# A mixture-of-experts kernel: one gather buffer, a scatter in native float32, 21 weight buffers for 19

## The chip, the core and the metric

One core of a Trainium2 chip. The metric is device time in microseconds (us), the median of several executions of the whole kernel. The engines named below are TensorE (PE in the rows; its weight loads are PEld), VectorE (DVE), ScalarE (ACT), GpSimd (POOL) and SyncE (SP), which issues nearly all of the weight transfers.

## What is computed

256 tokens of width 1024 go through two blocks. The first is attention (two kinds, merged through gates) and then a mixture of 32 experts. The second is three kinds of attention and a dense MLP. The change touches the mixture and the two rows that scale the first block's branches:

```python
mod_x = (jax.nn.silu(c) @ w_ada[l] + b_ada[l])[:, None, :]
sh_a, sc_a, g_a, sh_m, sc_m, g_m = jnp.split(mod_x, N_MOD, axis=-1)
x = x + g_a * _merge(ya, yb, ga, gb, w_oa[l], w_ob[l], w_out[l])
hx = _modulate(_rmsnorm(x, norm_mlp[l]), sh_m, sc_m)
x = x + g_m * moe(hx)
# moe: each token goes to 4 of the 32 experts, weighted by a softmax of its 4 largest logits
gate = jnp.minimum(xe @ w_gate[e] + b_gate[e], SWIGLU_LIMIT)
up = jnp.clip(xe @ w_up[e] + b_up[e], -SWIGLU_LIMIT, SWIGLU_LIMIT)
act = (up + 1) * (gate * jax.nn.sigmoid(SWIGLU_ALPHA * gate))
yb = act @ w_down[e] + b_down[e]
y = segment_sum(yb * weight, token)
```

Every expert has three matrices of 1024 x 1024 float32. All 96 of them are read, 4 MB each.

## The kernel before

The first block's attention fills the span up to about 300 us, the experts follow to about 1226 us, and the second block takes the rest. The function `moe()` holds the experts, two at a time: 16 pairs. Each expert has 64 slots for tokens, so the 128 rows of a PSUM bank hold two experts, the first in the array's columns 0 to 63, the second in 64 to 127 (`ab` = 0 and 1). What does not fit in 64 slots is done by `overflow()`, a branch behind pair 6 (`OVER_AT`) that these inputs do not enter, but whose count SyncE and the others have to read.

A weight tile is 1 MB, and a pair needs 24: eight each for gate, up and down. The tiles live in a ring of `SLOTS` = 12 buffers and in `EXTRA` = 7 more that exist only while the experts run. `fill()` issues a transfer (L206) as soon as a buffer is given back; which buffer that is, and which transfer, is fixed when the program is built.

For each pair `p` the loop at the end of `moe()` writes: `gate(p)`; the scatter of pair p-2; `prep1` and `prep2` of pair p+1; `up(p)`; `prep3` of pair p+1; `down(p-1)`; `trans(p)`. `prep1` builds a 0/1 matrix (scaled) on VectorE, and `prep2` gathers with it: 16 native float32 matmuls of 128 columns (L1291) put the pair's tokens into PSUM, and 4 ScalarE and 4 VectorE instructions (L1299, L1296) apply the norm and write the tile `xg`, which has two buffers. `prep3` transposes the 0/1 matrix (L1308) into the scatter's matrix `sc`, and finds the slots' weights `ws` (L1313). `expert_mm` (L1381) runs gate, up and down: for one pair of weight tiles it issues eight matmuls of 64 x 512, alternately in the one half of the array and in the other. Such a group of eight is called a block here; a pair has 12. Gate's and up's bias is a small matmul ahead (L1372).

`gate` clips (VectorE L1398), takes the sigmoid (ScalarE L1399) into a scratch tile of the name `e2` and multiplies (L1400). `up` clips into a scratch tile (L1409), and then adds one and multiplies (L1410). Down's result is split by ScalarE and VectorE (`split_out`, L513 and L514) into a rounded high part and the rest, and `scatter` (L1464, L1465) adds both with two matmuls in the reduced type float32r to the sum of the tokens, `acc`, for two halves of the tokens and two of the width: 8 matmuls of 128 x 512 for a pair. `acc` holds four of the eight PSUM banks from start to end; the other four rotate.

`tc.issue_after` and a scheduler settle the order on each engine: gathers and scatters are put between the matmuls of a block where their inputs are expected to be ready, so the order of the source is not that of the engine.

The row `gm_b` (g_m, copied to all partitions) is made during attention by `ada_one` and `bcast_rows` (L683 to L685), beside `ga_b`, and is used once, behind the experts (L1609).

## Time and profile before

| what | us |
|---|---|
| median of 3 runs (1702.76 to 1704.06) | 1703.26 |
| the profiled execution | 1698.37 |
| its span in the trace | 1696.6 |
| TensorE busy in it | 1621.6 (96%) |
| VectorE busy | 695.2 (41%) |
| ScalarE busy | 466.0 (27%) |
| experts, first gate bias to the last of them (in the trace) | 301.73 to about 1226 |

The profiled execution is 4.9 us below the median, and its span is 1.77 us shorter than its own time. The times in the rows below are of that span. "Busy" of TensorE contains time in which only one half of the array works, so 96% does not say that it could not go faster. A bracket in a row by time is idle time of the engine just before, and what ended it.

### The profile page before, as it was taken

How to read it: one execution, taken by the hardware profiler on the slowest of the kernel's cores; microseconds unless marked ns; L12 is line 12 of the kernel's file. 1: busy time of each engine (PE TensorE's matmuls, PEld its weight loads, DVE VectorE, ACT ScalarE, POOL GpSimd, SP SyncE). 2: the span in 40 equal slices, each digit the busy share in tenths (PEclk: the TensorE clock that was granted, in tenths of full speed). 3: DMA queues.
4: the chain of work that ended last, by engine and by line, in shares of the span. 5: the costliest groups of instructions: out<-in, count | busy, mean ns of one | idle time of the engine just before them, and what ended most of it. 6: DMA issues, size and time to landing. Idle time of an engine off the chain costs nothing. (4 is left out here: it accounts for less than half of the span.)

```text
span 1696.6 us, 22129 instructions
## 1 busy us (share of the span) xinstructions
PE 1621.6 (96%) x9024; PEld 1012.3 (60%) x9024; DVE 695.2 (41%) x1348; ACT 466.0 (27%) x768; POOL 81.8 (5%) x112
## 2 busy tenths in 40 slices
PE   5999899999999999899999999999999999999997
PEld 3777797544434443354344334433388899989996
DVE  4898986311121111221211111111267556665555
ACT  3435564101000100110000001000256445454443
POOL 2102100000000000000000000000004101100001
PEclk9999999999999999999999999999999999999999
DMA  9643588999999999999999999999973433565540
GB/s 344 260 154 141 202 282 335 382 425 425 426 426 425 425 425 426 382 425 425 425 426 425 425 426 426 426 422 424 405 277 102 146 121 131 178 218 184 176 153 25
DMA packets 117035, 537.42 MB, mean 317 GB/s; under 512 B 11666, under 2 KB 13438, under 8 KB 66754
## 3 DMA queue, kind: packets, MB, share of 16 engines
q1 hardware_dynamic: 112144, 532.19, 78.4%
q10 hardware_dynamic: 4610, 3.52, 0.7%
q8 instruction: 72, 1.18, 0.3%
q0 software_dynamic: 176, 0.26, 0.1%
q14 instruction: 33, 0.27, 0.0%
HBM read 534.88 MB, written 1.05 MB: 316 GB/s over the span
## 5 line engine op out<-in xcount | busy, mean ns | idle before, releaser
L1381 PE MATMUL bank_a<-w,xg 128*64 128x512 f32 x2048 | 522.5, 599 | 2.2 <-DMA w<-in_w_up_dram 2.2
L1381 PEld LDWEIGHTS bank_a<-w,xg 128*64 128x64 f32 x2048 | 182.7, 137 | 280.9 <-issue 258.5
L319 DVE TENSOR_TENSOR wl<-w,wh 128x1024 fp32r<-128x1024 f32 (+1 forms) x193 | 236.2, 1228 | 153.0 <-ACT wh L316 145.1
L316 ACT ACTIVATE wh<-w 128x1024 fp32r<-128x1024 f32 (+1 forms) x193 | 202.1, 1049 | 220.1 <-PE bank_a L389 98.7
L1381 PE MATMUL bank_a<-w,at 128*64 128x512 f32 x960 | 228.4, 595 | 6.5 <-DVE e L1409 5.0
L390 PE MATMUL bank_a<-hi,wl 128*128 128x256 f32 x640 | 180.3, 283 | 1.0 <-DVE wl L319 1.0
L388 PE MATMUL bank_a<-hi,wh 128*128 128x256 f32 x616 | 176.3, 287 | 1.1 <-ACT hi L474 0.6
L389 PE MATMUL bank_a<-lo,wh 128*128 128x256 f32 x616 | 174.3, 283 | 0.2 <-DVE lo L475 0.2
L1381 PEld LDWEIGHTS bank_a<-w,at 128*64 128x64 f32 x960 | 83.5, 137 | 146.6 <-issue 102.9
L513 ACT ACTIVATE y<-bank_a,ws 128x512 fp32r<-128x512 f32 x32 | 22.0, 687 | 443.1 <-PE bank_a L1381 429.9
L390 PEld LDWEIGHTS bank_a<-hi,wl 128*128 128x128 f32 x640 | 122.3, 192 | 1.4 <-DVE wl L319 1.4
L388 PEld LDWEIGHTS bank_a<-hi,wh 128*128 128x128 f32 x616 | 117.8, 192 | 3.2 <-issue 0.9
L389 PEld LDWEIGHTS bank_a<-lo,wh 128*128 128x128 f32 x616 | 118.1, 192 | 0.9 <-DVE lo L475 0.6
L514 DVE SCALAR_TENSOR_TENSOR y<-bank_a,ws,y 128x512 fp32r<-128x512 f32 x32 | 24.0, 751 | 217.9 <-ACT y L513 216.2
L1409 DVE TENSOR_SCALAR e<-bank_a 128x512 f32<-128x512 f32 x32 | 22.1, 691 | 187.1 <-PE bank_a L1381 185.9
L1399 ACT ACTIVATE e<-gs 128x512 f32<-128x512 f32 x32 | 20.2, 630 | 236.7 <-DVE gs L1398 225.2
L1291 PEld LDWEIGHTS bank_a<-gr,x_sb 128*128 128x128 f32 x512 | 64.2, 196 | 23.0 <-issue 19.5
L1398 DVE TENSOR_SCALAR gs<-bank_a 128x512 f32<-128x512 f32 x32 | 22.0, 691 | 131.2 <-PE bank_a L1381 115.8
L1291 PE MATMUL bank_a<-gr,x_sb 128*128 128x128 f32 x512 | 69.3, 286 | 0.7 <-DVE gr L1274 0.7
L1296 DVE TENSOR_SCALAR xg<-bank_a,abp 128x128 f32<-128x128 f32 x64 | 21.9, 404 | 107.7 <-PE bank_a L1291 107.5
L1299 ACT ACTIVATE xg<-bank_a,abp 128x128 f32<-128x128 f32 x64 | 24.2, 455 | 121.8 <-PE bank_a L1291 121.7
L354 PE MATMUL bank_b<-wh,hh 128*128 128x512 f32 x128 | 49.9, 390 | 0.0
(453 smaller groups left out, 2198.4 us busy)
## 6 DMA issues: line engine op xcount, KB each, us to landing
w<-in_w_up_dram SPq DMA_DIRECT2D x144, 1024.0 KB
w<-in_w_down_dram SPq DMA_DIRECT2D x136, 1024.0 KB
w<-in_w_gate_dram SPq DMA_DIRECT2D x128, 1024.0 KB
w<-in_w_in_dram SPq DMA_DIRECT2D x45, 1024.0 KB
w<-in_w_ada_dram SPq DMA_DIRECT2D x16, 1024.0 KB
w<-in_w_ada_dram SPq DMA_DIRECT2D x16, 512.0 KB
w<-in_w_out_dram SPq DMA_DIRECT2D x8, 1024.0 KB
w<-in_w_down_dram SPq DMA_DIRECT2D x16, 512.0 KB
```

The costliest lines, as they stand in the source:

```text
L316: split_last[0] = S.activation(r32(wh[:, :n]), t[:, o:o + n], AF.Copy)
L319: V.tensor_tensor(r32(wl[:, :n]), t[:, o:o + n], wh[:, :n], op=OP.subtract)
L354: PE.matmul(o, r32(sh), r32(mh), start=first, stop=False)
L388: PE.matmul(o, r32(wh[:, k, c]), r32(hi[:, j]), start=j == 0 and m % 2 == 0, stop=False)
L389: PE.matmul(o, r32(wh[:, k, c]), r32(lo[:, j]), start=False, stop=False)
L390: PE.matmul(o, r32(wl[:, k, c]), r32(hi[:, j]), start=False, stop=j == 7 and m % 2 == 1)
L513: S.activation(r32(hi), src, AF.Copy, scale=scale)
L514: V.scalar_tensor_tensor(out=r32(lo), in0=src, scalar=scale, in1=hi, op0=OP.mult, op1=OP.subtract)
L1291: PE.matmul(ps[:, k], x_sb[:, tt, o:o + 255:2], d["gr"][:, tt].rearrange("p e s -> p (e s)"), start=tt == 0, stop=tt == 1)
L1299: S.activation(xg[:, j], ps[:, k], AF.Identity, bias=abp_[:, 1, j:j + 1], scale=abp_[:, 0, j:j + 1])
L1381: state["mm"] = PE.matmul(ps[h][64 * ab:64 * ab + 64], lhs(j, ab), w[ab][:, e, 512 * h:512 * h + 512], start=bias is None and j == 0, stop ...
L1409: V.tensor_scalar(out=u_, in0=ps[h], scalar1=7.0, scalar2=-7.0, op0=OP.min, op1=OP.max)
```

## The change

- `EXTRA` goes from 7 to 9: 21 weight buffers while the experts run.
- The room comes from smaller scratch. `xg` has one buffer. The `e2` tiles are gone: gate's sigmoid is written back into its PSUM bank, and so is up's clip. `gm_b` is no longer kept from attention to the end.
- With one `xg`, the next pair's gather may not be written before `up(p)` has read the present one, so `prep1`, `prep2` and `prep3` of pair p+1 are written behind `up(p)` (behind `overflow()` for pair 6).
- `down_out` writes one float32 tile for a pair, half of it by ScalarE and half by VectorE, and `scatter` is one native float32 matmul where it was two of float32r: 4 for a pair.
- `gate_rows`, behind the experts, makes g_m's row anew: 8 native float32 matmuls of 128 x 128, 8 VectorE instructions ahead of them and 2 ScalarE copies behind. During attention, four matmuls and two copies for it are left out.
- Scratch pools of `overflow()` are rearranged.

```diff
-EXTRA = 7
+EXTRA = 9
...
-            xg = m2.tile([128, 8, 2 * CAP], F32, name="xg", tag="xg")
+            xg = m1.tile([128, 8, 2 * CAP], F32, name="xg", tag="xg")
...
-                s_ = m1.tile([128, 512], F32, name="e2", tag="e2")
                 V.tensor_scalar(out=g_, in0=ps[h], scalar1=7.0, scalar2=None, op0=OP.min)
-                S.activation(s_, g_, AF.Sigmoid, scale=1.702)
-                V.tensor_tensor(g_, g_, s_, op=OP.mult)
+                S.activation(ps[h], g_, AF.Sigmoid, scale=1.702)
+                V.tensor_tensor(g_, g_, ps[h], op=OP.mult)
...
-                V.tensor_scalar(out=u_, in0=ps[h], scalar1=7.0, scalar2=-7.0, op0=OP.min, op1=OP.max)
-                V.scalar_tensor_tensor(out=g_, in0=u_, scalar=1.0, in1=g_, op0=OP.add, op1=OP.mult)
+                V.tensor_scalar(out=ps[h], in0=ps[h], scalar1=7.0, scalar2=-7.0, op0=OP.min, op1=OP.max)
+                V.scalar_tensor_tensor(out=g_, in0=ps[h], scalar=1.0, in1=g_, op0=OP.add, op1=OP.mult)
...
         def down_out(p, h, ps):
-            y = scr([128, 1024], "y", "wl")
-            yh, yl = y[:, 0:512], y[:, 512:1024]
-            split_out(yh, yl, ps, pairs[p]["ws"])
-            state["y", p, h] = (yh, yl)
+            if ("ybuf", p) not in state:
+                state["ybuf", p] = scr([128, 1024], "y", "wl")
+            y = state["y", p, h] = state["ybuf", p][:, 512 * h:512 * h + 512]
+            ws = pairs[p]["ws"]
+            if h:
+                V.tensor_scalar(out=y, in0=ps, scalar1=ws, scalar2=None, op0=OP.mult)
+            else:
+                S.activation(y, ps, AF.Copy, scale=ws)
...
-                yh, yl = state.pop(("y", p, h))
+                y = state.pop(("y", p, h))
                 for tt in range(2):
-                    st_ = r32(sc[:, 128 * tt:128 * tt + 128])
-                    PE.matmul(acc[tt][h], st_, r32(yh), start=False, stop=False)
-                    PE.matmul(acc[tt][h], st_, r32(yl), start=False, stop=p == NPAIR - 1)
+                    PE.matmul(acc[tt][h], sc[:, 128 * tt:128 * tt + 128], y, start=False, stop=p == NPAIR - 1)
...
-            if p + 1 < NPAIR:
-                prep1(p + 1)
-                prep2(p + 1)
             if p == 0:
                 prep3(0)
             up(p)
-            if p + 1 < NPAIR:
+            if p + 1 < NPAIR and p != OVER_AT:
+                prep1(p + 1)
+                prep2(p + 1)
                 prep3(p + 1)
...
+                prep1(p + 1)
+                prep2(p + 1)
+                prep3(p + 1)
...
+        def gate_rows(h):
+            ps = bank("a", shape=(128, 4, 128))
+            for i in range(4):
+                dg = rest[:, h, 128 * i:128 * i + 128]
+                V.tensor_scalar(out=dg, in0=ident, scalar1=mod[:, 2, i, 2 + h, 0:1], scalar2=None, op0=OP.mult)
+                PE.matmul(ps[:, i], ones, dg, start=i == 0, stop=i == 3)
+            S.copy(gm_b[:, 512 * h:512 * h + 512], ps.rearrange("p i n -> p (i n)"))
```

TensorE, a pair in the middle of the experts (pair 3 to 5, 9 or later), from the end of the gate's bias. `w,xg` are gate's and up's matmuls, `y,sc` scatters, `gr,x_sb` gathers. Before:

```order
L1381 MATMUL bank_a<-w,xg 64x512 x2
L1464 MATMUL bank_b<-y,sc 128x512
L1381 MATMUL bank_a<-w,xg 64x512 x6
L1465 MATMUL bank_b<-y,sc 128x512
L1464 MATMUL bank_b<-y,sc 128x512
L1465 MATMUL bank_b<-y,sc 128x512
L1291 MATMUL bank_a<-gr,x_sb 128x128 x3
L1381 MATMUL bank_a<-w,xg 64x512 x2
L1291 MATMUL bank_a<-gr,x_sb 128x128 x7
L1381 MATMUL bank_a<-w,xg 64x512 x6
L1291 MATMUL bank_a<-gr,x_sb 128x128 x6
L1381 MATMUL bank_a<-w,xg 64x512 x2
```

In the changed kernel, the same stretch, the gate's first two blocks:

```order
L1377 MATMUL bank_a<-w,xg 64x512 x2
L1461 MATMUL bank_b<-y,sc 128x512
L1377 MATMUL bank_a<-w,xg 64x512 x6
L1461 MATMUL bank_b<-y,sc 128x512 x2
L1377 MATMUL bank_a<-w,xg 64x512 x2
```

and the rest of gate and up, from behind up's bias matmuls to prep3's first transpose (`kh,gb`):

```order
L1377 MATMUL bank_a<-w,xg 64x512 x24
L1287 MATMUL bank_a<-gr,x_sb 128x128 x7
L1377 MATMUL bank_a<-w,xg 64x512 x6
L1287 MATMUL bank_a<-gr,x_sb 128x128 x6
L1377 MATMUL bank_a<-w,xg 64x512 x2
L1287 MATMUL bank_a<-gr,x_sb 128x128 x3
L1377 MATMUL bank_a<-w,xg 64x512 x22
L1304 LDWEIGHTS gb
L1304 MATMUL bank_a<-kh,gb 128x128
```

The scatter still stands inside gate's first block, one matmul where there were two. Of the 16 gathers, seven stood inside one block (gate's second) and nine between blocks; now seven stand inside up's first block, three inside its second and six between them. Each time they stand between two matmuls of one half of the array and two of the other. Prep3 has moved from between gate and up to between up and down.

VectorE, the end of up and the begin of down in such a pair: L1409 and L1410 are up's clip and product, L514 is down's result. Before:

```order
L1409 TENSOR_SCALAR e_4079<-bank_a 128x512
L1410 SCALAR_TENSOR_TENSOR gs<-e_4079,gs 128x512
L1409 TENSOR_SCALAR e_4082<-bank_a 128x512
L1410 SCALAR_TENSOR_TENSOR gs<-e_4082,gs 128x512
L514 SCALAR_TENSOR_TENSOR y<-bank_a,ws,y 128x512 x2
L1317 TENSOR_REDUCE ws<-bank_a 64x1 x2
L1310 CAST sc<-bank_a 128x256
```

In the changed kernel (L1403 and L1404 are up's clip and product, L1292 the gather's write of `xg`, L1424 half of down's result):

```order
L1403 TENSOR_SCALAR bank_a<-bank_a 128x512
L1404 SCALAR_TENSOR_TENSOR gs<-bank_a,gs 128x512
L1403 TENSOR_SCALAR bank_a<-bank_a 128x512
L1292 TENSOR_SCALAR xg<-bank_a,abp 128x128
L1404 SCALAR_TENSOR_TENSOR gs<-bank_a,gs 128x512
L1292 TENSOR_SCALAR xg<-bank_a,abp 128x128 x3
L1273 TENSOR_TENSOR gb<-kc,pos 128x256
L1424 TENSOR_SCALAR y<-bank_a,ws 128x512
L1313 TENSOR_REDUCE ws<-bank_a 64x1 x2
L1306 CAST sc<-bank_a 128x256
```

The four writes of `xg` now stand among up's clip and product, ahead of everything that prep3 and down give VectorE.

## Rows read from the trace of the kernel before

**Rows 1.** Page, part 2: GB/s moved, 40 equal slices of the span.
```profile
GB/s 344 260 154 141 202 282 335 382 425 425 426 426 425 425 425 426 382 425 425 425 426 425 425 426 426 426 422 424 405 277 102 146 121 131 178 218 184 176 153 25
```

**Rows 2.** By windows: length; busy and counts of PE, PEld, DVE, ACT, POOL; clock; DMA; GB/s.
```profile
301.73:389.69 87.96, 86.50 (x434) 42.39 (x434) 21.17 (x54) 9.82 (x18) 0.00 (x0) 0.98 0.97 405
389.69:448.69 59.00, 57.94 (x255) 23.77 (x254) 10.28 (x22) 5.31 (x10) 0.00 (x0) 1.00 1.01 425
448.69:506.93 58.24, 57.18 (x255) 23.25 (x254) 10.28 (x22) 5.31 (x10) 0.00 (x0) 1.00 1.01 425
623.44:688.63 65.19, 58.18 (x258) 23.89 (x257) 10.14 (x21) 5.89 (x11) 0.00 (x0) 0.99 1.01 425
688.63:849.68 161.05, 159.91 (x753) 71.65 (x753) 31.22 (x70) 15.23 (x29) 0.00 (x0) 0.98 0.99 414
849.68:1143.17 293.49, 287.85 (x1261) 117.77 (x1261) 49.83 (x104) 26.54 (x50) 0.00 (x0) 1.00 1.01 425
```

**Rows 3.** By windows: two stretches of 10 us with little transfer.
```profile
300.00:310.00 10.00, 10.00 (x58) 4.50 (x58) 3.58 (x14) 2.14 (x4) 0.00 (x0) 1.00 0.66 247
700.00:710.00 10.00, 10.00 (x64) 5.96 (x62) 3.25 (x6) 2.65 (x6) 0.00 (x0) 1.00 0.63 243
```

**Rows 4.** Waits of SyncE's DMA queue, 310 to 680 us: total us, times, longest.
```profile
SPq L206 <- PE bank_a L1381: 231.4, 98, 8.4
```

**Rows 5.** TensorE by time, one pair: start, us, line, tile, count, [idle before].
```profile
456.54 1.93 PE L1381 MATMUL bank_a<-w,xg 128*64 128x512 f32 x4
458.40 1.92 PE L1291 MATMUL bank_a<-gr,x_sb 128*128 128x128 f32 x14
460.25 3.65 PE L1381 MATMUL bank_a<-w,xg 128*64 128x512 f32 x12
...
474.17 0.28 PE L1308 MATMUL bank_a<-kh,gb 128*128 128x128 bf16 x2
475.02 0.25 PE L1313 MATMUL bank_a<-w,gb 128*128 128x96 bf16 x2 [0.56 <-DVE gs L1398]
475.19 14.01 PE L1381 MATMUL bank_a<-w,xg 128*64 128x512 f32 x64
489.13 1.07 PE L1381 MATMUL bank_a<-w,at 128*64 128x512 f32 x2
490.65 13.95 PE L1381 MATMUL bank_a<-w,at 128*64 128x512 f32 x62 [0.45 <-DVE e L1409]
504.53 0.73 PE L1464 MATMUL bank_b<-y,sc 128*128 128x512 f32 x2
```

**Rows 6.** TensorE by time near the end of the experts.
```profile
1201.02 3.69 PE L1359 MATMUL bank_b<-bd,wtt 32*128 32x512 f32 x8
1204.64 0.50 PE L1464 MATMUL bank_b<-y,sc 128*128 128x512 f32 x1
1204.97 0.39 PE L1465 MATMUL bank_b<-y,sc 128*128 128x512 f32 x1
1205.20 0.39 PE L1464 MATMUL bank_b<-y,sc 128*128 128x512 f32 x1
1205.43 0.40 PE L1465 MATMUL bank_b<-y,sc 128*128 128x512 f32 x1
```

**Rows 7.** VectorE by time where up ends and down begins.
```profile
488.38 0.69 DVE L1409 TENSOR_SCALAR e<-bank_a 128x512 f32<-128x512 f32 x1 [11.43 <-PE bank_a L1381]
...
490.63 0.69 DVE L1410 SCALAR_TENSOR_TENSOR gs<-e,gs 128x512 f32<-128x512 f32 x1
```

**Rows 8.** Instructions by line and form, 400 to 640 us: busy, mean ns.
```profile
L514 DVE SCALAR_TENSOR_TENSOR y<-bank_a,ws,y 128x512 fp32r<-128x512 f32 x8 | 6.0, 751 | 53.2 <-ACT y L513 52.7
...
L1296 DVE TENSOR_SCALAR xg<-bank_a,abp 128x128 f32<-128x128 f32 x16 | 5.5, 404 | 38.7 <-PE bank_a L1291 38.7
```

**Rows 9.** TensorE by time, first matmul after the overflow's branch.
```profile
688.63 1.06 PE L1372 MATMUL bank_a<-b_gate,sel 96*64 96x512 bf16 x4 [5.95 <-PEq L1473]
```

**Rows 10.** TensorE by time, the last pair's waits for weights (two of four).
```profile
1177.75 2.79 PE L1381 MATMUL bank_a<-w,xg 128*64 128x512 f32 x10 [1.65 <-DMA w<-in_w_up_dram]
...
1197.44 2.79 PE L1381 MATMUL bank_a<-w,at 128*64 128x512 f32 x10 [0.61 <-DMA w<-in_w_down_dram]
```

More of the change, by code (lines that the diff above doesn't have):

```diff
@@ L430, in build @@
     mod = keep.tile([128, 3, 4, 4, 2], F32, name="mod")
-    gm_b = keep.tile([128, D], F32, name="gm_b")
     kc = keep.tile([128, 256], F32, name="kc")
@@ L527, in body @@
         ga_b = p1.tile([128, D], F32, name="ga_b")
+        gm_s = p1.tile([128, D], F32, name="gm_s")
         rwa = p1.tile([128, 8, 32], F32, name="rwa")
@@ L620, in ada_one @@
             w = live[("ada", g, j)]
-            for c, acc in enumerate((ga_b, gm_b)):
+            for c, acc in enumerate((ga_b, gm_s)):
                 o = slice(1024 * c, 1024 * c + 1024)
@@ L632, in ada_one @@
             for c in range(4):
-                PE.matmul(ps[32 * c:32 * c + 32], one_row, (ga_b, gm_b)[c // 2][:, 512 * (c % 2):512 * (c % 2) + 512],
+                PE.matmul(ps[32 * c:32 * c + 32], one_row, (ga_b, gm_s)[c // 2][:, 512 * (c % 2):512 * (c % 2) + 512],
                           start=True, stop=True)
@@ L656, in ada_one @@
                 late["row"] = grow
-            if g == 2:
-                add_row(mrow, 2, mrow, 1)
-                late["rows"] = mrow
         ada_step.append(ada_one)
@@ L1084, in body @@
             ada_one()
-        spreads = bcast_rows(ga_b, 0, late["row"]), bcast_rows(gm_b, 2, late["rows"])
+        spreads = [bcast_rows(ga_b, 0, late["row"])]
         yb_hi, yb_lo = late["yb"][:, 0], late["yb"][:, 1]
@@ L1131, in body @@
                 if (h, q) == (0, 0):
-                    for f in spreads:
-                        f()
+                    spreads[0]()
             for b in range(2):
@@ L1309, in prep3 @@
             sc = m2.tile([128, T], F32, name="sc", tag="sc")
-            V.tensor_copy(r32(sc), ps)
+            V.tensor_copy(sc, ps)
             pw = bank("a", shape=(128, 3, 32))
@@ L1486, in overflow @@
                     ev = nc.sync.value_load(ei[0:1, 0:1], min_val=0, max_val=NE - 1)
-                    one = m1.tile([128, 32], F32, name="one")
                     V.tensor_scalar(out=one, in0=iota[:, :32], scalar1=eb[:, 0:1], scalar2=None, op0=OP.is_equal)
-                    jk2 = m1.tile([128, 32], F32, name="jk2")
                     for tt in range(2):
@@ L1529, in block_bias @@
                     def block_bias(nm, h):
-                        t = scr([64, 512], "bb", "wl")
-                        nc.sync.dma_start(out=t, in_=sl[nm][bass.ds(ev, 1), 512 * h:512 * h + 512].to_broadcast([64, 512]))
-                        return t
+                        t = scr([64, 1024], "bb", "wl")
+                        nc.sync.dma_start(out=t[:, 0:512],
+                                          in_=sl[nm][bass.ds(ev, 1), 512 * h:512 * h + 512].to_broadcast([64, 512]))
+                        return t[:, 0:512], t[:, 512:1024]
                     for h in range(2):
-                        ps = block_mm("gate", lambda j: xo[:, j], h)
-                        bt = block_bias("b_gate", h)
-                        g_ = m1.tile([64, 512], F32, name="e2", tag="e2")
-                        V.tensor_tensor(g_, ps, bt, op=OP.add)
+                        g_ = block_mm("gate", lambda j: xo[:, j], h)
+                        bt, s_ = block_bias("b_gate", h)
+                        V.tensor_tensor(g_, g_, bt, op=OP.add)
                         V.tensor_scalar(out=g_, in0=g_, scalar1=7.0, scalar2=None, op0=OP.min)
-                        s_ = scr([64, 512], "s_", "wl")
                         S.activation(s_, g_, AF.Sigmoid, scale=1.702)
@@ L1553, in overflow @@
                     for h in range(2):
-                        s = slice(512 * h, 512 * h + 512)
                         ps = block_mm("down", lambda j: ato[:, j], h)
@@ L1589, in moe @@
         parts = new_parts()
+        gm_b, rest = big("gm_b")[:, :D], big3("rest", 4)
+        def gate_rows(h):
[5 more added lines that the diff above has]
+            S.copy(gm_b[:, 512 * h:512 * h + 512], ps.rearrange("p i n -> p (i n)"))
+        for h in range(2):
+            gate_rows(h)
         ps_k = last = None
```

24 lines of the change are left out of this document (11 added, 13 removed).

## The prediction

> **What bounds the kernel now.** I read the transfers first. From the ninth slice to the 28th the core moves 422 to 426 GB/s, but for one slice of 382 [rows 1], so while the experts run the weights come as fast as this trace shows them coming at all. A pair is 24 tiles of 1 MB, 25.17 MB, and at 0.4255 MB per us that is 59.15 us. Then I read the same stretch as TensorE sees it. A pair of the steady kind takes 58.24 us, with TensorE busy for 57.18 of them [rows 2]. So TensorE's own work for a pair is only 0.9 us shorter than its weights: two limits lie side by side. Who waits for whom tells which one is ahead: from 310 to 680 us SyncE's queue stood for 231.4 us until TensorE had given a buffer back [rows 4], so there TensorE, eating the stock of full buffers, sets the pace. Only in the last pair does TensorE wait for weights, four times, of which the longest (1.65 us) and the last (0.61) stand in [rows 10] and the other two are 0.5 each, 3.3 us together. The transfers have two dips, each 10 us at some 245 GB/s instead of 425, about 4.2 us lost each: at 300, when all 19 buffers are full, and at 700, behind the branch of the overflow [rows 3]. At that branch TensorE stood for 5.95 us [rows 9], which makes the pair around it 65.19 us long [rows 2].
>
> That decides how the change is to be read. More TensorE time in a pair is free up to 0.9 us; what is above that goes into the end. More buffers help only while weights are what is waited for.
>
> **The change part by part**, against the profiled execution of 1698.37 us.
>
> *Scatter.* Eight float32r matmuls start 0.23 us apart (1204.97, 1205.20, 1205.43) [rows 6]: 1.87 us for a pair. A native float32 matmul of 128 x 512 does not occur before. The nearest are four with 32 rows, eight records in the 3.62 us from 1201.02 to 1204.64, 0.905 each [rows 6], and the experts' own 64 x 512, of which 32 take 13.94 us two at a time (475.19 to 489.13), 0.87 each [rows 5]. So four cost 3.48 to 3.62, and the change adds 1.6 to 1.75 us for a pair; I take 1.65. ScalarE and VectorE have less to do at down's result, but they are not waited for there.
>
> *Blocks that are broken.* A block of eight alternates between the halves of the array and takes 13.94/4 = 3.49 us unbroken [rows 5]. With gathers inside, its first two matmuls (one half alone) take 1.86 us from 456.54 to 458.40, and the other six start at 460.25 and last 3.65 [rows 5]; less the gathers in between that is some 5.45 us, so a break costs 1.95 beside the instructions that stand in it. Before, a pair has two such blocks (scatter, gathers). In the new order it has three: the scatter's, and two of up's by gathers. Up's bias stands inside a block in both. That adds 1.95 a pair; the bounds are 0, if the halves go on filling each other, and 2.0. The Trainium skill (TensorE: Matmul & The Clock Gate, section The mechanism, in its part on packing small matmuls) says of matmuls that they are "pc-monotone in start AND end", a strict FIFO in which only different tiles of the array overlap. By that rule a break turns four steps into six, an estimate of 2 x 0.87 = 1.74 us for 1.95, and the sum below would be some 2 us lower.
>
> *Up to down.* VectorE's clip starts at 488.38, and its last product of up at 490.63; down's second matmul starts at 490.65, after 0.45 us idle, released by the second clip [rows 5, 7]. In the new order a PSUM bank becomes free only with the product (the clip stays in the bank), and four writes of `xg`, which can't start before up has read the old one, stand among these: one ahead of the last product, three behind it. With products of 0.75 us (the row with a PSUM source) and writes of 0.40 [rows 8], the chain from the second clip's end at about 490.6 is 0.40 + 0.75 + 3 x 0.40, to about 493; by the shortest gaps 492.75. Down's first matmuls are queued on TensorE behind prep3, which needs a bank too, and all 32 behind the first. So down's second start moves from 490.65 to 492.75 or 493.1: +2.1 to +2.5, taken as 2.1. Bounds: 0, if banks come free sooner than I read, and 4.0, if gathers and prep3 wait one after another. Against that, prep3's 1.02 us between gate and up (474.17 to 475.19) [rows 5] falls into this wait: -1.02. In the stretch from down to the next gate (504.53 to 506.93) [rows 2, 5] one scatter stands where four stood, and some waiting for down's result goes: -0.4 (0 to -0.6).
>
> *Sum of a steady pair.* 1.65 + 1.95 + 2.1 - 1.02 - 0.4 = +4.28, so 62.5 us. That is above 59.15: the experts become bound by TensorE. Pairs 3 to 5 (three of 58.24): +12.8. Pairs 10 to 14 now take 293.49 [rows 2]; five of 62.5 are 312.6: +19.1. Pair 2 (59.00) has its gathers outside the blocks: +2.4. Pairs 0 and 1 (87.96 together) have no scatter and gathers outside the blocks: 0 (bounds -1, +2). Pairs 7 to 9 (161.05) lack one scatter, and begin with full buffers: +4.6 (0 to 12). Pair 6: TensorE is later by then, the transfers are not, so most of its 5.95 us at the branch go, but pair 7's gather and prep3 stand uncovered behind it: some -5 + 3 = -2 (bounds -5, +4). Together +36.9.
>
> *Behind them.* In pair 15 the waits for weights go (-3.3); three scatters still come (3 x 1.65 = 4.95) and one break (1.95); `gate_rows` has 8 matmuls of 128 x 128, its VectorE and ScalarE instructions in one chain: 2.0, between 0, if it fits into down's last waits, and 4. Together about +5.5. During attention the spread of `gm_b` goes, four short matmuls: -0.9 (0 to -1). The sigmoid in PSUM, one instruction of 0.6 us on ScalarE, stands beside gate's and up's 28 us of matmuls; it costs nothing unless banks become scarce, and that is the wait priced above.
>
> *The two buffers.* The first two tiles of 1 MB more fill the first dip (4.2 us of weights earlier). TensorE doesn't wait for weights there, so it is worth 0 as long as TensorE is the limit.
>
> Sum: 36.9 + 5.5 - 0.9 = +41.5, so 1739.9 for an execution like the profiled one. The median lay 4.9 us above the profiled execution; with the same distance **1744 us**.
>
> **The rivals.** *The pair stays at or below its weights* (the other side). The mechanism: the additions run in TensorE's idle half. If breaks cost nothing and the chain from up to down is covered, a pair is 58.24 + 1.65 - 1.02 = 58.9, below 59.15, and that figure is the point from which it decides. Then the end is set by the last weights. The first dip is filled (-4.2), the second perhaps as well (-4.2), against +5.5 + 3.3 behind the last weights (no waits go) less 0.9: 1698.4 - 8.4 + 7.9 = 1697.9, a median of about 1703, between 1698 (`gate_rows` and one scatter hidden) and 1707. For it speaks that before TensorE stands only 0.9 us from its weights, so little is missing; against it that the broken block is plainly in the rows. The Trainium skill (Trainium Kernel Development and Optimization, section Best Practices) advises to "overlap DMA with compute" by double buffering, and by it more weight buffers would speak for this case and one gather buffer against it; rows 4 and 10 agree with it only in the last pair.
>
> *One of the two terms is absent.* If the chain from up to down is covered by free banks, a pair is 62.5 - 2.1 = 60.4; if the breaks cost nothing, 60.6. Either takes about 2 us from nine or ten pairs and the ends of the others: 1744 - 22 = 1722. For it speaks that gathers and prep3 themselves stand in the wait; against it that only four banks rotate.
>
> *More waiting.* Gathers in up need two banks that gate's product must have left, and every write of `xg` waits for up's end. If they serialise by one more product and clip (1.4 us) in each of 12 pairs: 1744 + 17 = 1761.
>
> *The change doesn't do what it says:* the two buffers fill once and then only shift the queue. That is already in my sum, at 0.
>
> **How the numbers follow.** My forecast, 1744 (1732 to 1755 by the bounds of its terms): 0.55. One term absent, about 1722 (1712 to 1732): 0.22. More waiting, 1755 to 1770: 0.13. The pair stays below its weights, 1698 to 1707: 0.10. The range reaches from 1716 to 1763; it leaves out the last case and a tail of the third. A measurement of this kernel can tell about 0.2%, 3.4 us, from no change. Of the last case about two thirds end within that and a third below: faster 0.03, same 0.07, slower 0.90.
>
> **What would show it.** The begins of gate's bias should lie some 62.5 us apart in pairs 3 to 5 and 10 to 14, GB/s between them should fall from 425 to about 403, and SyncE should wait for TensorE to the end. Scatter's records: eight for a pair, 0.43 us apart. Two blocks of up's with gathers inside, at 5.4 us each. Down's second matmul some 2 us later after up's end than now, with VectorE's write of `xg` as the releaser. No wait for weights in the last pair, and none of 5.95 us at the branch. I am wrong if a pair takes less than 59.2 us, if TensorE still waits for weights in pairs 13 to 15, or if what is lost stands in one place that is not among these, such as attention or the second block.

## The result and the profile after

The changed kernel is slower: 1721.87 us median (1720.34 to 1728.74, six runs) beside 1702.87 for the kernel before in the same comparison, a ratio of 1.0128 (95% interval 1.0114 to 1.0141), some 19 us. The forecast was 1744, some 41 us; the sign was right, the size was twice too large, and the measured time lies near the rival in which one of two terms is absent, about 1722. The two profiled executions lie 23 us apart, more than the medians, because that of the kernel before is a quick one: 4.5 us below its median here, where the changed kernel's is 0.6 below.

The profiled execution of the changed kernel took 1721.30 us, its span is 1719.6. The transfers in 40 slices (page, part 2), to be set beside [rows 1]:

```profile
GB/s 345 252 172 144 190 301 308 425 424 424 425 424 426 425 425 424 382 426 425 424 424 425 424 426 425 424 425 333 315 261 114 123 123 148 170 211 176 178 161 25
```

They still run at 424 to 426 GB/s through the middle of the experts, but fall to 333 and 315 in the 28th and 29th slice, where the kernel before had 424 and 405. The transfers stop there for a reason that the prediction did not have. SyncE's last transfers of expert weights (L219) wait for the landing of another one, that of down's bias `bd` (total us, times, longest):

```profile
SPq L219 <- DMA bd<-in_b_down_dram: 21.3, 1, 21.3
```

`bd` takes a buffer of `xg`, of which there is now one. So it is issued at 1199.6 us, behind the last up, where the kernel before issued it at 1124.1; SyncE's next transfer starts at 1201.7, and from 1195 to 1200 the core moves 18 GB/s. Why SyncE waits for that landing these traces do not tell. No matmul waits for it: TensorE's waits below name no weight transfer.

TensorE's view of the pairs, by windows (length; busy and counts of PE, PEld, DVE, ACT, POOL; granted clock; DMA share; GB/s), to be set beside [rows 2]; first pair 2, then pair 3, pair 6, and pairs 10 to 14:

```profile
383.72:446.62 62.90, 60.79 (x254) 25.93 (x254) 9.32 (x21) 4.57 (x9) 0.00 (x0) 0.97 1.01 425
446.62:507.82 61.20, 59.09 (x254) 25.54 (x254) 9.32 (x21) 4.57 (x9) 0.00 (x0) 1.00 1.01 425
631.54:696.15 64.61, 60.82 (x259) 32.84 (x258) 8.35 (x17) 5.06 (x10) 0.00 (x0) 0.95 1.01 424
857.43:1163.43 306.00, 295.46 (x1262) 127.61 (x1261) 45.00 (x99) 22.85 (x45) 0.00 (x0) 1.00 1.01 425
```

A steady pair takes 61.20 us for 58.24, and the five pairs 10 to 14 exactly five times that. Set against the kernel before, the start of the first pair is 2.9 us earlier (298.80 for 301.73), pairs 0 and 1 are 3.0 shorter, pair 2 is 3.9 longer, pairs 3 to 5 are 10.2 longer, pair 6 is 0.6 shorter, pairs 7 to 9 are 0.2 longer, pairs 10 to 14 are 12.5 longer, and from the last pair's gate to the end it is 2.7 longer (556.17 for 553.43). The sum is the 23.0 us between the two spans. The 2.9 us ahead of the experts can't be put down to the change: kernels that share the changed kernel's code up to there have their first gate anywhere from 298.8 (this one) to 304.2 (a_whole_19).

One steady pair by time (start, us, line, tile, count, [idle before and what ended it]), to be set beside [rows 5]; L1377 are the experts' matmuls, L1461 the scatter, L1287 the gathers, L1304 and L1309 prep3:

```profile
447.07 1.88 PE L1377 MATMUL bank_a<-w,xg 128*64 128x512 f32 x4
448.88 1.12 PE L1461 MATMUL bank_b<-y,sc 128*128 128x512 f32 x2
449.94 3.65 PE L1377 MATMUL bank_a<-w,xg 128*64 128x512 f32 x12
453.52 1.98 PE L1461 MATMUL bank_b<-y,sc 128*128 128x512 f32 x4
455.43 1.07 PE L1377 MATMUL bank_a<-w,xg 128*64 128x512 f32 x2
...
457.45 10.65 PE L1377 MATMUL bank_a<-w,xg 128*64 128x512 f32 x46
468.52 1.89 PE L1287 MATMUL bank_a<-gr,x_sb 128*128 128x128 f32 x14 [0.42 <-DVE gs L1395]
470.34 3.65 PE L1377 MATMUL bank_a<-w,xg 128*64 128x512 f32 x12
473.91 1.68 PE L1287 MATMUL bank_a<-gr,x_sb 128*128 128x128 f32 x12
475.52 1.93 PE L1377 MATMUL bank_a<-w,xg 128*64 128x512 f32 x4
477.38 0.97 PE L1287 MATMUL bank_a<-gr,x_sb 128*128 128x128 f32 x6
478.29 10.51 PE L1377 MATMUL bank_a<-w,xg 128*64 128x512 f32 x44
489.46 0.28 PE L1304 MATMUL bank_a<-kh,gb 128*128 128x128 bf16 x2 [0.66 <-DVE gs L1404]
490.40 0.24 PE L1309 MATMUL bank_a<-w,gb 128*128 128x96 bf16 x2 [0.65 <-ACT xg L1295]
491.02 14.86 PE L1377 MATMUL bank_a<-w,at 128*64 128x512 f32 x64 [0.38 <-PE bank_a L1309]
505.81 0.74 PE L1415 MATMUL bank_a<-ident,gs 128*128 128x128 f32 x4
```

Three blocks are broken by full-width matmuls, as the order showed: 447.07 (scatter), the end of 457.45 to 470.34 (gathers), 475.52 (gathers). Behind up there are three short waits (0.66, 0.65 and 0.38) where there was one of 0.45. VectorE at that place, beside [rows 7]:

```profile
487.98 0.70 DVE L1403 TENSOR_SCALAR bank_a<-bank_a 128x512 f32<-128x512 f32 x1 [8.60 <-PE bank_a L1377]
488.71 0.69 DVE L1404 SCALAR_TENSOR_TENSOR gs<-bank_a,gs 128x512 f32<-128x512 f32 x1
...
489.92 0.40 DVE L1292 TENSOR_SCALAR xg<-bank_a,abp 128x128 f32<-128x128 f32 x1
...
490.84 1.04 DVE L1292 TENSOR_SCALAR xg<-bank_a,abp 128x128 f32<-128x128 f32 x3
```

TensorE waits (engine, line, what for: us in total, times, longest) from 300 to 1300 us:

```profile
PE bank_a L1304 <- DVE gs L1404: 6.6, 10, 0.7
PE bank_a L1309 <- ACT xg L1295: 6.5, 10, 0.7
PE bank_a L1287 <- DVE gs L1395: 4.3, 10, 0.6
```

They lead the list, and nothing in it names a transfer of expert weights: the waits of [rows 10] are gone, and so are the 5.95 us of [rows 9].

### The profile page after: what moved, and what is told of

Read it like the earlier page. It is cut to its first block, busy times and chain, and to the rows that moved or that the text cites. A ratio compares the mean times of both kernels' runs of the same rounds, so it can differ in the third digit from the quotient of the medians.

```text
span 1719.6 us, 22157 instructions
## 1 busy us (share of the span) xinstructions
PE 1637.9 (95%) x9036; PEld 1040.2 (60%) x9036; DVE 680.3 (40%) x1337; ACT 453.0 (26%) x751; POOL 81.4 (5%) x112
## 4 chain that ended last, share of the span: by engine, by line
PE 56%; DVE 2%; ACT 1%; issue 1%; POOL 0%; ACTq 0%; DVEq 0%
PE bank_a L1377 24%; PE bank_a L388 4%; PE bank_a L390 4%; PE bank_a L389 4%; PE bank_a L1287 2%; PE bank_b L1461 2%; PE bank_b L354 2%; PE bank_b L355 2%; PE bank_b L356 2%; PE bank_a L1446 1%; PE bank_a L355 1%; PE bank_a L356 1%; PE bank_a L354 1%; DVE wl L319 1%; PE bank_a L1895 1%
## 5 line engine op out<-in xcount | busy, mean ns | idle before, releaser
L1377 PE MATMUL bank_a<-w,xg 128*64 128x512 f32 x2048 | 516.9, 595 | 0.0
L1377 PEld LDWEIGHTS bank_a<-w,xg 128*64 128x64 f32 x2048 | 211.5, 136 | 261.9 <-issue 200.0
L1377 PE MATMUL bank_a<-w,at 128*64 128x512 f32 x960 | 226.6, 601 | 3.8 <-PE bank_a L1309 2.3
L1377 PEld LDWEIGHTS bank_a<-w,at 128*64 128x64 f32 x960 | 80.9, 138 | 136.1 <-issue 122.9
L1295 ACT ACTIVATE xg<-bank_a,abp 128x128 f32<-128x128 f32 x64 | 24.2, 457 | 280.1 <-PE bank_a L1377 204.2
L1424 DVE TENSOR_SCALAR y<-bank_a,ws 128x512 f32<-128x512 f32 x16 | 12.0, 750 | 208.5 <-PE bank_a L1377 207.0
L1394 ACT ACTIVATE bank_a<-gs 128x512 f32<-128x512 f32 x32 | 19.2, 601 | 282.0 <-DVE gs L1393 282.0
L1403 DVE TENSOR_SCALAR bank_a<-bank_a 128x512 f32<-128x512 f32 x32 | 22.2, 695 | 176.9 <-PE bank_a L1377 176.9
L1287 PEld LDWEIGHTS bank_a<-gr,x_sb 128*128 128x128 f32 x512 | 65.5, 202 | 37.7 <-issue 31.8
L1287 PE MATMUL bank_a<-gr,x_sb 128*128 128x128 f32 x512 | 72.1, 294 | 8.5 <-DVE gs L1395 4.3
L1426 ACT ACTIVATE y<-bank_a,ws 128x512 f32<-128x512 f32 x16 | 11.0, 688 | 250.8 <-PE bank_a L1377 250.8
L1461 PE MATMUL bank_b<-y,sc 128*128 128x512 f32 x128 | 64.8, 616 | 0.2 <-DVE y L1424 0.2
L1306 DVE CAST sc<-bank_a 128x256 f32<-128x256 bf16 x16 | 6.8, 422 | 123.2 <-PE bank_b L1461 123.2
```

What stands on the lines that cost most here:

```text
L1287: PE.matmul(ps[:, k], x_sb[:, tt, o:o + 255:2], d["gr"][:, tt].rearrange("p e s -> p (e s)"), start=tt == 0, stop=tt == 1)
L1295: S.activation(xg[:, j], ps[:, k], AF.Identity, bias=abp_[:, 1, j:j + 1], scale=abp_[:, 0, j:j + 1])
L1377: state["mm"] = PE.matmul(ps[h][64 * ab:64 * ab + 64], lhs(j, ab), w[ab][:, e, 512 * h:512 * h + 512], start=bias is None and j == 0, stop ...
L1461: PE.matmul(acc[tt][h], sc[:, 128 * tt:128 * tt + 128], y, start=False, stop=p == NPAIR - 1)
```

## Experiments

The ratio is against the kernel before on the same chip, whose median there was 1700.65 to 1702.87; "pair" is the distance of two gate biases in pairs 3 to 5.

| kernel | us, median | ratio (95%) | pair, us |
|---|---|---|---|
| before | 1702.87 | 1 | 58.24 |
| changed | 1721.87 | 1.0128 (1.0114 to 1.0141) | 61.20 |
| a_split | 1705.20 | 1.0025 (1.0014 to 1.0037) | 58.45 |
| b_native | 1726.63 | 1.0161 (1.0140 to 1.0183) | 60.28 |
| a_order | 1740.87 | 1.0240 (1.0223 to 1.0258) | 62.23 |
| a_19 | 1725.65 | 1.0146 (1.0129 to 1.0163) | 61.20 |
| a_whole | 1711.55 | 1.0069 (1.0047 to 1.0091) | 52.43, later 59.1 |
| a_whole_19 | 1707.41 | 1.0044 (1.0029 to 1.0059) | 52.43, later 59.0 |
| b_whole | 1700.18 | 0.9999 (0.9985 to 1.0012) | 52.44, later 59.0 |
| whole_split | 1706.65 | 1.0029 (1.0013 to 1.0044) | 58.3 |
| b_order | 1704.06 | 1.0022 (1.0005 to 1.0039) | 58.38 |
| b_psum | 1711.87 | 1.0073 (1.0047 to 1.0100) | 60.19 |
| b_rows | 1703.05 | 1.0024 (1.0011 to 1.0037) | 58.25 |
| best | 1696.99 | 0.9982 (0.9968 to 0.9997) | 52.45, later 59.0 |

**a_split**: the changed kernel with the old scatter.

```diff
-                    PE.matmul(acc[tt][h], sc[:, 128 * tt:128 * tt + 128], y, start=False, stop=p == NPAIR - 1)
+                    PE.matmul(acc[tt][h], st_, r32(yh), start=False, stop=False)
+                    PE.matmul(acc[tt][h], st_, r32(yl), start=False, stop=p == NPAIR - 1)
```

> The changed kernel with down's result split again into a float32r high part and rest, and the scatter as eight float32r matmuls; all else as changed (21 buffers, one gather buffer, new order, sigmoid in PSUM, row at the end). Theory: the native float32 scatter is the main cost, by its own time (+1.35 us a pair with the stretch behind down, as the two traces show) and because an instruction of twice the length stands inside a block. Then the pair falls from 61.2 to 58.5 to 59.2 us, back at what the weights allow (59.15), and the time to 1703 to 1708. Rival: the new order (gathers inside up, one gather buffer, the wait between up and down) is the main cost. Then the pair stays at 60 us or more, and the time falls by no more than 8 us, to 1714 or above.

The pair is 58.45 us and the time 1705.2: the theory's numbers. The gate of that kernel by time, and its way from up to down:

```profile
449.47 3.65 PE L1377 MATMUL bank_a<-w,xg 128*64 128x512 f32 x16
453.06 0.74 PE L1459 MATMUL bank_b<-y,sc 128*128 128x512 f32 x2
...
487.52 0.29 PE L1304 MATMUL bank_a<-kh,gb 128*128 128x128 bf16 x2 [0.66 <-DVE gs L1404]
488.45 0.24 PE L1309 MATMUL bank_a<-w,gb 128*128 128x96 bf16 x2 [0.65 <-ACT xg L1295]
489.08 14.86 PE L1377 MATMUL bank_a<-w,at 128*64 128x512 f32 x64 [0.38 <-PE bank_a L1309]
```

Two of the eight scatters stand behind gate's first block, which is whole (16 records in 3.59 us), and the others behind down. So going from native to float32r takes away the broken block (1.9 us), 0.2 us of the gathers' wait, and only 0.7 us of scatter and what stands beside it: 0.66 us in gate and 3.62 behind down (503.88 to 507.50) for 2.97 and 2.01. The larger part of what this edit gains is the order that comes with it. The three short waits of the new order are all still there (0.66, 0.65, 0.38).

**b_native**: the kernel before with the native scatter alone (the diff the other way round, with the one y tile for a pair).

> The kernel before with one part of the change alone: the native float32 scatter with its one float32 tile for a pair. 19 buffers, two gather buffers, the old order. Theory (scatter is the main cost): the pair goes from 58.24 to 60.3 to 60.8, so TensorE becomes the limit, and the time to 1717 to 1722. Rival (the order is the main cost): the pair to at most 59.2, hidden behind the weights, and the time within 4 us of before.

The pair is 60.28, just below what the theory wanted; the time is 1726.6, above it, and more than the whole change costs. Of the 25 us some 9 lie behind the experts, in one row:

```profile
PE bank_a L388 <- ACT tail L316: 9.0, 1, 9.0
```

The second block's first matmuls waited for ScalarE, whose rounding of their weights was queued behind a sum of squares that waited for the experts' result. That is an accident of that kernel's order; the pairs 0 to 14 together are 18.2 us longer (859.7 for 841.4).

**a_order**: the changed kernel in the old order, with two gather buffers and, for room, 20 weight buffers.

```diff
-EXTRA = 9
+EXTRA = 8
...
-            xg = m1.tile([128, 8, 2 * CAP], F32, name="xg", tag="xg")
+            xg = m2.tile([128, 8, 2 * CAP], F32, name="xg", tag="xg")
...
+            if p + 1 < NPAIR:
+                prep1(p + 1)
+                prep2(p + 1)
             up(p)
-            if p + 1 < NPAIR and p != OVER_AT:
-                prep1(p + 1)
-                prep2(p + 1)
+            if p + 1 < NPAIR:
                 prep3(p + 1)
```

> The changed kernel with two gather buffers and the old place of the next pair's gather and of prep3 (between gate and up); to make room 20 weight buffers for 21. Native scatter, sigmoid in PSUM and the row at the end stay. Theory (scatter is the main cost): the pair falls from 61.2 by the 0.65 us that the traces give to the way from up to down, and by at most 0.5 for the bank that the gathers wait for, to 60.1 to 60.6, and the time by 5 to 12 us, to 1710 to 1717. Rival (the order is the main cost): the pair falls to 59.2 or less, and the time to 1702 to 1706.

Both lost: 62.23 us a pair and 1740.9 in all, 19 us slower than the changed kernel. So the new order is not a cost; with the rest of the change it saves 19 us. In a_order prep3 stands inside up's first block, and the gathers break two blocks. Why prep3 stands there, b_psum shows.

**b_psum**: the kernel before with the sigmoid and the clip in PSUM and nothing else.

```diff
-                S.activation(s_, g_, AF.Sigmoid, scale=1.702)
-                V.tensor_tensor(g_, g_, s_, op=OP.mult)
+                S.activation(ps[h], g_, AF.Sigmoid, scale=1.702)
+                V.tensor_tensor(g_, g_, ps[h], op=OP.mult)
```

> The kernel before with one part of the change alone: gate's sigmoid and up's clip written back into PSUM, no scratch tiles for them. In its order prep3 stands inside up's first block, two matmuls behind its begin, where it stood between gate and up. Theory: a broken block costs 1.9 us wherever it comes from, so the pair goes from 58.24 to 59.8 to 61 us (two kernels that differ by just this, native scatter with and without it, are 62.23 and 60.28), TensorE becomes the limit, and the time goes to 1708 to 1720. Rival: the sigmoid in PSUM is off the path, as I took it: 58.3 us and within 3 us of before.

60.19 us a pair and +0.73% are the theory's numbers, but its reason does not hold. Around prep3 (L1308, L1313) and at down's begin, beside [rows 5] at 474.17 and 489.13:

```profile
467.42 7.03 PE L1381 MATMUL bank_a<-w,xg 128*64 128x512 f32 x31
475.40 0.29 PE L1308 MATMUL bank_a<-kh,gb 128*128 128x128 bf16 x2 [0.95 <-DVE gs L1399]
476.16 0.26 PE L1313 MATMUL bank_a<-w,gb 128*128 128x96 bf16 x2 [0.47 <-DVE gs L1399]
...
491.00 1.04 PE L1381 MATMUL bank_a<-w,at 128*64 128x512 f32 x2 [0.71 <-PE bank_a L1381]
492.38 13.95 PE L1381 MATMUL bank_a<-w,at 128*64 128x512 f32 x62 [0.33 <-DVE gs L1408]
```

Prep3 waits 0.95 and 0.47 us for gate's last product (L1399), since the bank with the sigmoid is free only then, and the scheduler has put it two matmuls later, into up's first block. Prep3 with its waits takes 0.88 us more than before (474.45 to 476.35), and down's second matmul comes 2.09 us behind up's end (490.29) for 1.52, so 0.57 more. That leaves 0.49 of the 1.95 us for the broken block, not 1.9: the theory's number came out by luck. In the prediction I took the sigmoid in PSUM as free unless banks become scarce. In the old order sigmoid and clip in PSUM cost 1.95 us a pair; in the new one, where prep3 is behind up, 0.4 are seen in the waits of L1287 for L1395 above, and prep3's 0.66 for up's product may be another part.

**b_order** (the kernel before with one gather buffer and the new order) and **b_rows** (with the row made at the end):

```diff
-            xg = m2.tile([128, 8, 2 * CAP], F32, name="xg", tag="xg")
+            xg = m1.tile([128, 8, 2 * CAP], F32, name="xg", tag="xg")
```

> The kernel before with one part of the change alone: one gather buffer, and the next pair's gather and prep3 behind up. 19 buffers, float32r scatter, scratch tiles for sigmoid and clip. TensorE's order has as many broken blocks as before (scatter, gathers, bias). Theory: the new order costs a pair only the wait between up and down, 0 to 0.7 us, so 58.2 to 58.9, which the weights (59.15) hide: 1699 to 1705. Rival: the one gather buffer is itself a cost: a pair of 60 us or more, 1712 or above.

> The kernel before with one part of the change alone: the MLP gate's row made behind the experts, its spread during attention left out. Theory: its 1.95 us of TensorE lie behind the last weights, and 0.9 us go during attention: 0 to 3 us slower, 1700 to 1704. Rival: hidden in the waits of the last matmuls: 0.5 to 1.5 us faster.

b_order has pairs of 58.38 us, below the weights, and +0.22%, both as expected: in this order the one gather buffer is nearly free. Its way from up to down takes 17.08 us (484.84 to 501.92) for 15.40 before, as in the changed kernel; but up's bias falls between two blocks here and costs 1.0 us where it cost 1.76, and prep3 no longer stands between gate and up. b_rows costs +0.24%, 2.4 us, within its theory's range; its trace does not show where, since pair 7 is 5.6 us longer there (57.71 for 52.15) and the stretches ahead of the experts and behind them are shorter. The four parts alone add up to 1.61 + 0.73 + 0.22 + 0.24 = 2.8%, some 0.5 of it b_native's accident, and the change has 1.28%: they are not independent, since each moves the order on TensorE for the others.

**a_19**: the changed kernel with EXTRA = 7.

> The changed kernel with 19 weight buffers for 21. Theory: no matmul in the changed kernel waits for weights, so the two buffers are worth nothing: the pair stays at 61.2 and the time within 0.2% (3.4 us) of the changed kernel's 1722. Rival: they fill the dip at 300 us and the changed kernel needs that: the time goes up by 4 to 8 us, with waits for weights in the trace.

The pair is 61.20 as with 21, no wait for weights appears, and the ratio (1.0129 to 1.0163) overlaps the changed kernel's (1.0114 to 1.0141). The estimates lie 0.18%, 3 us, apart, just inside the theory's 3.4; that the two buffers are worth anything is not shown.

**a_whole**: the changed kernel with TensorE's groups tied one behind the other (`tc.issue_after` of the last matmul of the group ahead), so that no block is broken.

```diff
+        def behind(f, *args):
+            with tc.issue_after(state["mm"].ins):
+                f(*args)
...
-                scatter(p - 2)
+                behind(scatter, p - 2)
...
-            up(p)
+            behind(up, p)
...
-                prep2(p + 1)
-                prep3(p + 1)
+                behind(prep2, p + 1)
+                behind(prep3, p + 1)
```

> The changed kernel with TensorE's order fixed so that nothing stands inside a block: gate's 32 matmuls, the four native scatters, up's bias and its 32 matmuls, 16 gathers, prep3, down's 32 matmuls, 8 transposes, then the next pair. All else as changed. Theory: the changed kernel loses its time to blocks that are broken by other matmuls (scatter in gate, bias, two groups of gathers in up) and to the wait between up and down that whole groups would cover. Pair 1 of the changed kernel has this order already, without a scatter, and takes 48.98 us; with four scatters at 0.95 us a pair would be 52 to 53.5 us of TensorE, below the 59.15 of its weights. Then the weights set the end, native scatter and the one gather buffer cost nothing, and the time is 1698 to 1706. Rival: native scatter costs its own time wherever it stands, and the blocks matter little: pairs of 59.5 us or more, 1713 or above.

The pair by time:

```profile
438.26 0.62 PE L1369 MATMUL bank_a<-b_gate,sel 96*64 96x512 bf16 x4
438.71 13.96 PE L1378 MATMUL bank_a<-w,xg 128*64 128x512 f32 x64
452.60 3.70 PE L1462 MATMUL bank_b<-y,sc 128*128 128x512 f32 x8
...
456.68 13.96 PE L1378 MATMUL bank_a<-w,xg 128*64 128x512 f32 x64
470.57 4.04 PE L1288 MATMUL bank_a<-gr,x_sb 128*128 128x128 f32 x32
...
474.73 14.43 PE L1378 MATMUL bank_a<-w,at 128*64 128x512 f32 x64
...
490.69 0.62 PE L1369 MATMUL bank_a<-b_gate,sel 96*64 96x512 bf16 x4
```

52.43 us from gate bias to gate bias (438.26 to 490.69): the same work as in the changed kernel's 61.20, with the native scatter's 3.63 us in one piece. From pair 5 on TensorE waits for weights and the pair is 59.1. So 8.8 us of a pair of the changed kernel are nothing but order, breaks and waits together. The time is 1711.55, above the 1698 to 1706 I expected; the cause is behind the last weights, which come at the same moment as before. First a_whole, then the changed kernel, from the last block of pair 14's down (L1378, L1377) to down of pair 15 (L1447, L1446):

```profile
1197.38 3.65 PE L1378 MATMUL bank_a<-w,at 128*64 128x512 f32 x12 [0.60 <-DMA w<-in_w_down_dram]
1200.95 4.31 PE L1357 MATMUL bank_b<-bd,wtt 32*128 32x512 f32 x8
1205.20 1.98 PE L1416 MATMUL bank_a<-ident,gs 128*128 128x128 f32 x8
1206.97 5.46 PE L1462 MATMUL bank_b<-y,sc 128*128 128x512 f32 x8
1212.28 1.95 PE L1601 MATMUL bank_a<-rest,ones 128*128 128x128 f32 x16
1214.15 2.37 PE L1447 MATMUL bank_a<-w,at 128*64 128x512 f32 x10
```

```profile
1202.32 13.95 PE L1377 MATMUL bank_a<-w,at 128*64 128x512 f32 x60
1216.19 3.69 PE L1355 MATMUL bank_b<-bd,wtt 32*128 32x512 f32 x8
1219.82 3.70 PE L1461 MATMUL bank_b<-y,sc 128*128 128x512 f32 x8
1223.36 1.95 PE L1592 MATMUL bank_a<-rest,ones 128*128 128x128 f32 x16
1225.23 1.08 PE L1446 MATMUL bank_a<-w,at 128*64 128x512 f32 x4
```

In the kernel before, the last block that waited for weights starts at 1197.44 [rows 10] and down of pair 15 at 1206.68. In a_whole it starts at 1197.38, and down of pair 15 at 1214.15, 7.5 us later: transposes, a scatter that is now native and 1.9 us of `gate_rows` lie there, partly at the lower clock (0.72 granted from 1201 to 1213). Behind the last weights the native scatter and the row are paid in full in both kernels. Another 4.4 us lie behind that point: from the begin of pair 15's down to the end of the span a_whole takes 494.4 us, as does the changed kernel, and the kernel before 489.9. Half of them come before the last scatter; for the other half, in the second block, no run here names the cause.

**a_whole_19**, **b_whole** and **whole_split**: the same ties with 19 buffers; in the kernel before; and in the changed kernel with float32r scatter.

```diff
-EXTRA = 9
+EXTRA = 7
```

> The same whole blocks with 19 weight buffers for 21. Theory: where the weights are the limit the two buffers count: the transfers stop at 300 us for want of a buffer, some 4 us of weights, so 2 to 5 us slower than with 21. Rival: the limit is not the weights, or the stop is made up for elsewhere: within 1.5 us of the run with 21.

> The kernel before with whole blocks: gate's 32 matmuls, eight float32r scatters, 16 gathers, up's 32, prep3, down's 32, 8 transposes. 19 buffers, two gather buffers. Theory: the kernel before was bound by its weights at the end (waits of 3.3 us in the last pair) and by TensorE in the middle, so TensorE's pair falls from 58.24 to 51 to 53 us and waits for weights, and the time by 0 to 5 us, to 1696 to 1702. Rival: TensorE bound it: 10 us or more are won.

> Whole blocks and the float32r scatter in the changed kernel (21 buffers, one gather buffer). Theory: as the run with whole blocks and native scatter, within 3 us: 1696 to 1705, since scatter's 1.6 us a pair lies in TensorE's wait for weights; only the last three scatters, behind the last weights, can give up to 4 us. Rival: 8 us or more faster than with native scatter.

b_whole is the clearest: TensorE's pair falls by 5.8 us, from 58.24 to 52.44, and the time does not move (0.9999, 0.9985 to 1.0012). So TensorE's pairs did not bound the kernel before; its weights did. What TensorE wins up to pair 5 it gives back at the branch of the overflow (pairs 6 and 7 take 134.8 us for 117.3), and from pair 10 on it waits for weights. a_whole_19 was to be slower than a_whole, and is if anything faster (1707.41 for 1711.55; the intervals overlap). The expected gain of two buffers did not show even where weights are the limit. In all these kernels the last transfer of expert weights is issued 976 to 977 us behind the first (976.0 before and in a_whole, 976.6 in a_whole_19, 976.8 in b_whole). In a_whole the 50th is issued 133.6 us behind the first for 140.5, but by the 200th, behind the branch, the lead is lost (510.0 for 509.3). Nor is it the two buffers that take away the dip at 300 us: from 300 to 310 us a_19, with 19, moves 409 GB/s, the changed kernel 417 and the kernel before 247, and in the first two the transfers are low ahead of it instead (115 and 174 GB/s from 280 to 290, for 324). whole_split misses its range by 1.7 us, and its distance from a_whole is 4.9 us where at most 3 were expected. Its order came out otherwise (gate's second bias waits 2.20 us for the product that frees its bank), with pairs of 58.3, so it does not test its theory.

**best**: b_whole with down's bias product (3.6 us) moved from behind the last weights to ahead of pair 15's up.

```diff
+            if p == NPAIR - 1:
+                behind(lambda: down_bias()())
             behind(up, p)
...
-            else:
-                bias_products = down_bias()
...
-            if p == NPAIR - 1:
-                with tc.issue_after(state["mm"].ins):
-                    bias_products()
```

> The kernel before with whole blocks, and down's bias product moved from behind the last weights of pair 14's down to ahead of pair 15's up, where TensorE waits for weights anyway. Theory: the end is set by the last weights and by what TensorE does behind them, so taking 3.6 us from behind them gives 2 to 4 us: 1696 to 1699. Rival: the end is set otherwise: the same as whole blocks alone, 1700.

1696.99 us, 0.9982 (0.9968 to 0.9997): some 3 us less than either kernel it comes from, and the only one here whose interval lies below the kernel before. The gain is at the edge of what this measurement tells. Beside b_whole the traces show it: down of pair 15 begins at 1206.47 for 1210.35. Beside the kernel before they do not (1206.68, and spans of 1696.4 and 1696.6): its profiled execution is the quick one.

## Why the prediction was right in sign and wrong in size

- **Two limits side by side** (58.24 of TensorE beside 59.15 of weights): right. b_whole shows that less TensorE time gains nothing, and in the changed kernel's pairs 10 to 14 five times 2.96 make 14.8, of which 12.5 are paid. But [rows 4] doesn't tell who is ahead, as I read it: beside its 231.4 us, the changed kernel's pairs of 61.20 give 231.8 with 19 buffers (a_19) and 114.3 with 21, all at 425 GB/s. And pair 14 had a wait for weights too, 0.35 us, which I passed over.
- **Scatter**: 1.65 a pair less 0.4 behind down, 1.25 together; measured 1.35. In gate three native matmuls take 1.06 + 1.91 = 2.97 us (448.88, 453.52) where four of float32r took 1.23; behind down the stretch is 2.01 for 2.40. Right.
- **Broken blocks**: this step failed. I took each break at 1.95 and added one. A break that stands alone has that price: the scatter's and the gathers' block take 1.9 us too much in the rows of both kernels. But breaks in one run of blocks are not added up one by one. Before, the block with up's bias in it and the one behind it took 8.74 us (465.43 to 474.17) for two blocks of 3.49, 1.76 too much (some 0.45 of it the bias itself, by a_whole), and the gathers' block 5.43, 1.94 too much. After, bias and first gathers follow each other in one run of whole blocks, from 455.43 to 468.10 and 470.34 to 473.91: 16.24 us for four blocks, 2.28 too much for both instead of 3.70. b_psum has the same: bias and prep3 stand in a run of six blocks that takes 9.23 + 13.94 us, 2.2 too much for both. With the second gathers (1.9) and the scatter (1.9) the changed kernel's breaks cost 6.1 us a pair, where the old ones cost 5.6: +0.5, and +0.42 of waiting for a bank, for the +1.95 forecast. My reading, from these rows alone: the first break leaves one half of the array half a step ahead, the run goes on overlapped in that shift, and the second break ends it. The Trainium skill states that matmuls start and end in order (TensorE: Matmul & The Clock Gate, The mechanism). The trace agrees for the starts: the records of the two matmuls ahead of the scatter start at 447.07 to 448.36, 0.43 apart, and the scatter follows at 448.88. I should have walked through the whole run with that rule, not through one block.
- **Up to down**: +2.1 less 1.02 for prep3, so +1.08. From up's end to down's end it is 17.01 us (488.80 to 505.81) for 15.40 (489.13 to 504.53): +1.61 less 1.02, +0.6. The chain is only in part the one described. Prep3 waits for up's product (L1404) and for ScalarE's write of `xg` (L1295), and down for prep3's last matmul (L1309); VectorE's writes of `xg`, which I named as the releaser, end none of these waits. VectorE was faster too: its product with a source in PSUM took 0.68 where I had put 0.75, and the writes of `xg` followed each other in 0.32.
- **Sum of a steady pair**: 0.9 + 0.6 + 1.35 = 2.85 by these, 2.96 measured, 4.28 forecast. Over pairs 3 to 5 and 10 to 14 that is 22.7 us measured for 31.9. The 4.9 us from the profiled execution to the median, which I carried over, came out as 0.6.
- **Pairs 0, 1 and 7 to 9**: forecast +4.6, measured -2.8. Pairs 1 and 7 have whole blocks in both kernels, but for gate's bias in pair 7 now, so there is little to break; the 4.6 that I put on pairs 7 to 9 was worked out from no row. Pairs 8 and 9 are 1.2 and 1.9 us longer, pair 7 is 2.9 shorter. Besides, the kernel before ran pair 1 and pair 7 at a granted clock of 0.97 and 0.95, and the changed kernel has such dips in pairs 2, 5 and 6 instead; these runs don't separate how much of the -2.8 that makes.
- **Behind the experts**: forecast +5.5 (its terms add up to 5.6), measured +2.7. From pair 15's gate to the begin of its down it is 1.7 us less (61.80 for 63.51), with 1.9 for `gate_rows` (1223.36 to 1225.23) in it: the waits for weights had gone, as foretold. Behind that it is 4.4 more, as said of a_whole.
- **The two buffers at 0**: nothing speaks against it, neither a_19 nor, where weights are the limit, a_whole_19. That they fill the dip at 300 us was wrong (a_19).
- **The rows that were to show it**: the waits for weights and the 5.95 us are gone, scatter has 8 records, and two of up's blocks have gathers inside, as foretold. GB/s did not fall to 403 between, and SyncE waited less for TensorE (114.3 us for 231.4 from 310 to 680). The second is the two buffers' doing, since a_19 has 231.8. For the first, a count of transfers and matmuls gives the likely reason. A steady pair adds 2.05 us of weights to the stock, and the short pairs 7 and 8 (49.25 and 51.87 us) take more from it: SyncE is 21 tiles ahead at the begin of pair 7, 15 at that of pair 9, and 18 at that of pair 15, so behind the branch a buffer is always free.
- **The rivals**: the one on the other side fell, since a pair of 61.20 is above 59.15. The one whose time was met, about 1722 with one term absent, did not come true either: both terms are there, each at about half its size. That its number fits is luck. Of the 18.5 us that the profiled executions lack of the forecast 41.5, steady pairs make 9.2 and pairs 0, 1 and 7 to 9 make 7.4.

## What to carry to other kernels

Before pricing an instruction that moves, see between which matmuls it lands: a full-width matmul between the two halves of a column-tiled block cost 1.9 us here beside its own time where it stood alone, two breaks in one run of blocks cost 2.3 together, and whole groups in a plain order were worth 8.8 us of a 61.2 us pair. Where two limits lay within 2%, less work on the one gained nothing and more work on it was paid almost at once; then what lay behind the last transfer counted (3.6 us moved ahead of it gave some 3). The parts of this change didn't add up (2.8% alone, 1.28% together), so test them in the order that the whole has. A shared buffer can delay something far from it: for want of a second `xg`, down's bias was fetched behind pair 15's up and no longer during pair 14.

## What was unexpected of the hardware

TensorE's granted clock fell in places where TensorE had waited. In best, behind waits of 0.57 us for weights and 1.22 for the bias's operand, up of pair 15 took 16.35 us for 64 records that take 13.9 else. By windows (columns as above), the stretch with up's begin and the one behind it:

```profile
1166.00:1190.00 24.00, 23.29 (x79) 8.39 (x81) 1.66 (x4) 0.00 (x0) 0.00 (x0) 0.79 1.01 426
1190.00:1205.00 15.00, 15.00 (x75) 7.09 (x72) 3.24 (x5) 2.13 (x4) 0.00 (x0) 1.00 1.02 403
```

0.79 of the full clock is a mean: part of the stretch at 1.2 GHz (0.50 from 1170 to 1175 us), the rest at 2.4. In a_whole the stretch from 1201 to 1213 had 0.72, and its four native scatters there took 5.31 us where the changed kernel's took 3.54. Waiting alone does not explain it: the kernel before waited 3.3 us for weights in its last pair and was granted 1.00 throughout from 1145 to 1250 us, and the changed kernel's pair 2, with no wait for weights, was granted 0.97.
